# A temperature softmax: the first four-row piece moved to the Scalar queue

## The chip, the cores and the metric

One Trainium2 chip, one of its cores. The metric is the time of one execution in device microseconds, measured on the chip. "Span" is the shorter time that the profile covers, from the core's first to its last instruction (161.2 us where the measured time is 163.27 us). Engines are named as in the profile: DVE is VectorE, ACT is ScalarE, SP is SyncE; SPq and ACTq are the instructions with which SP and ACT issue DMA transfers.

## The reference

The input is 16 x 1024 rows of 512 float32; each row gets a softmax at temperature 0.5.

```python
x_scaled = x / 0.5
x_max = np.max(x_scaled, axis=-1, keepdims=True)
exp_x = np.exp(x_scaled - x_max)
return (exp_x / np.sum(exp_x, axis=-1, keepdims=True)).astype(np.float32)
```

Read once and written once, that is 33.55 MB in and 33.55 MB out.

## The kernel before

The 16,384 rows are cut into 8 tiles of 4 MB: 128 partitions, each with 16 rows (32 KB that lie together in memory). A tile is worked in four blocks of four rows. There are six tile buffers. The first tile is loaded in two pieces, four rows and twelve rows, so that DVE need not wait for the whole tile. All loads are issued by SP, all stores by ACT.

```python
G = 16; B = 4; N_ACT = 1
FIRST = [(0, 4), (4, 16)]
data = ctx.enter_context(tc.tile_pool(name="data", bufs=6))
...
warm = stats.tile([P, 1], fp32, name="warm", bufs=1)     # loads ACT's table early
nc.vector.memset(warm, 0.0)
nc.scalar.activation(out=warm, in_=warm, func=EXP)
...
def load(c):
    xt = tiles[c] = data.tile([P, G, D], fp32, name="xt")
    for lo, hi in FIRST if c == 0 else [(0, G)]:
        nc.sync.dma_start(out=xt[:, lo:hi, :], in_=xr[c][:, lo:hi, :])

def shift(i):          # DVE: row maxima of a block, L65; bias = -2 * max, L67
    ...
def exponentials(i):   # ACT: four times exp(2 x + bias) with row sums, L74
    ...
def scale_vector(i):   # DVE: reciprocal of the sums, L87; three of four rows scaled, L89
    ...
def scale_scalar(i):   # ACT: the fourth row scaled, L95
    ...
def store(i):
    c, b = blocks[i]
    if b + B == G:
        nc.scalar.dma_start(out=outr[c], in_=tiles[c])

for i in range(n + 3):                 # n = 32 blocks
    if i < n:
        if blocks[i][1] == 0:
            load(blocks[i][0])
        shift(i); exponentials(i)
    if 1 <= i <= n:     scale_vector(i - 1)
    if 2 <= i <= n + 1: scale_scalar(i - 2)
    if 3 <= i:          store(i - 3)
```

## Time and profile before

| | before |
|---|---|
| time, median of the first 3 runs | 162.96 us |
| DVE, ACT busy, share of the span | 74%, 71% |
| data moved, mean rate over the span | 67.1 MB, 416 GB/s |
| first maximum on DVE starts | 5.43 us |
| first store issued / last store issued | 34.23 / 144.50 us |

These are the DMA row and the sum line of the page of the kernel before. In the row, each digit is the busy share (tenths, 9 is 90% or more) of one fortieth of the span.

```profile
DMA  5999999998999999999999999999999999999991
HBM read 33.55 MB, written 33.55 MB: 416 GB/s over the span
```

There is no stretch between the first microseconds and the last in which the DMA engines rest. The trace's packet records tell how near to full this is: a 32 KB packet takes 1.213 us, the packet times add up to 156.9 us for each of the 16 engines, and the first data packet starts at 1.76 us and the last ends at 159.94 us. So the engines are busy for 156.9 of 158.2 us.

The waits view of the kernel before (who waited for what: total us, times, longest) says what this means for DVE: it waits for loads.

```profile
DVE negmax L65 <- DMA xt<-in_x_dram: 19.8, 5, 4.8
```

Here is the page's list of DMA issues of the kernel before: destination and source, issuing queue, count, size of each, and the median time from issue to landing. The 1 MB piece lands 4.7 us after its issue.

```profile
xt<-in_x_dram SPq DMA_DIRECT2D x7, 4096.0 KB, 47.3
xt<-in_x_dram SPq DMA_DIRECT2D x1, 3072.0 KB, 11.5
xt<-in_x_dram SPq DMA_DIRECT2D x1, 1024.0 KB, 4.7
```

The timeline of the kernel before has start, duration, engine, line, operation, and in brackets the idle time before it with what ended it. DVE starts block 0 at 5.43 us and then idles 4.79 us for the second piece. The last two lines are the first and the last store.

```profile
5.43 2.29 DVE L65 TENSOR_REDUCE negmax<-xt 128x4 f32<-128x2048 f32 x1 [4.58 <-DMA xt<-in_x_dram]
...
12.71 2.29 DVE L65 TENSOR_REDUCE negmax<-xt 128x4 f32<-128x2048 f32 x1 [4.79 <-DMA xt<-in_x_dram]
...
16.51 2.28 DVE L65 TENSOR_REDUCE negmax<-xt 128x4 f32<-128x2048 f32 x1
...
34.23 0.37 ACTq L102 DMA_DIRECT2D out_dram<-xt  x1
...
144.50 0.34 ACTq L102 DMA_DIRECT2D out_dram<-xt  x1
```

### The profile page before, as it was taken

Reading aid. Unit: us, or ns where it says so; the run is one execution under the profiler, and the core shown is the slowest. Engines: PE = TensorE matmul, PEld = TensorE weight load, DVE = VectorE, ACT = ScalarE, POOL = GpSimd, SP = SyncE. Lnnn points to the kernel's source line nnn. Section 1 sums busy time; section 2 is a strip of 40 time slices with the busy share of each in tenths; the row PEclk is TensorE's granted clock in tenths of the full one; section 3 lists DMA queues with packets and bytes.
Section 4 is the critical chain, followed back from the end, with each engine's and each line's share of the span. In section 5 each row is a group of like instructions: output and inputs, shape, how many; then the busy total and the mean of one; then the engine's idle time right before and its main releaser. Section 6 shows DMA issues by size and latency. Waiting matters only on the chain.

```text
span 161.2 us, 563 instructions
## 1 busy us (share of the span) xinstructions
DVE 119.7 (74%) x193; ACT 114.8 (71%) x290; POOL 0.2 (0%) x4
## 2 busy tenths in 40 slices
DVE  0608999999999999999994999359991799930000
ACT  3072799999999998999995799809997199980000
POOL 0000000000000000000000000000000000000000
DMA  5999999998999999999999999999999999999991
GB/s 193 457 463 447 390 463 447 392 455 317 417 472 398 431 472 398 423 480 398 423 472 409 390 488 423 390 488 423 390 488 423 390 488 425 390 480 431 390 480 65
DMA packets 2452, 67.14 MB, mean 416 GB/s; under 512 B 272, under 2 KB 272, under 8 KB 272
## 3 DMA queue, kind: packets, MB, share of 16 engines
q1 hardware_dynamic: 1296, 33.56, 49.2%
q10 hardware_dynamic: 1152, 33.55, 48.2%
q14 instruction: 4, 0.03, 0.0%
HBM read 33.55 MB, written 33.55 MB: 416 GB/s over the span
## 4 chain that ended last, share of the span: by engine, by line
DMA 54%; DVE 31%; ACT 3%; issue 1%; SPq 0%
DMA xt<-in_x_dram 36%; DVE negmax L65 19%; DMA out_dram<-xt 18%; DVE xt L89 10%; ACT xt L74 2%; DVE bias L67 1%; ACT xt L95 1%; DVE recip L87 1%; SPq L59 0%
## 5 line engine op out<-in xcount | busy, mean ns | idle before, releaser
L74 ACT ACTIVATE xt<-xt,bias 128x512 f32<-128x512 f32 x128 | 90.8, 710 | 28.9 <-DVE bias L67 28.9
L65 DVE TENSOR_REDUCE negmax<-xt 128x4 f32<-128x2048 f32 x32 | 73.0, 2281 | 19.8 <-DMA xt<-in_x_dram 19.8
L89 DVE TENSOR_SCALAR xt<-xt,recip 128x512 f32<-128x512 f32 x96 | 40.9, 483 | 1.1
L74 ACT ACTIVATION_READ_ACCUMULATOR xt<-xt,bias 128x1 f32 x128 | 23.9, 187 | 0.0
L95 ACT ACTIVATE xt<-xt,recip 128x512 f32<-128x512 f32 x32 | 22.4, 706 | 0.0
L87 DVE RECIPROCAL recip<-sums 128x4 f32<-128x4 f32 x32 | 5.5, 171 | 1.6 <-ACT xt L74 1.6
L67 DVE TENSOR_SCALAR bias<-negmax 128x4 f32<-128x4 f32 x32 | 5.5, 170 | 1.1
L50 ACT ACT_TABLE_LOAD x1 | 1.3, 1283 | 0.7 <-PEq L131 0.7
L49 DVE MEMSET warm<- 128x1 f32 x1 | 0.1, 59 | 0.8 <-PEq L131 0.8
L50 ACT ACTIVATE warm<-warm 128x1 f32<-128x1 f32 x1 | 0.2, 203 | 0.0
L131 POOL MEMSET const-bfloat16-1.0<- 128x1 bf16 x1 | 0.1, 101 | 0.0
L131 POOL MEMSET const-uint8-127<- 128x1 uint8 x1 | 0.1, 101 | 0.0
L131 POOL MEMSET const-float32-0.0<- 128x1 f32 x1 | 0.1, 98 | 0.2 <-issue 0.2
L131 POOL MEMSET const-float32-1.0<- 128x1 f32 x1 | 0.1, 98 | 0.0
## 6 DMA issues: line engine op xcount, KB each, us to landing
out_dram<-xt ACTq DMA_DIRECT2D x8, 4096.0 KB, 26.9
xt<-in_x_dram SPq DMA_DIRECT2D x7, 4096.0 KB, 47.3
xt<-in_x_dram SPq DMA_DIRECT2D x1, 3072.0 KB, 11.5
xt<-in_x_dram SPq DMA_DIRECT2D x1, 1024.0 KB, 4.7
```

Source lines behind the costliest of these rows:

```text
L49: nc.vector.memset(warm, 0.0)
L50: nc.scalar.activation(out=warm, in_=warm, func=EXP)
L65: nc.vector.tensor_reduce(negmax, xb, axis=AX, op=MAX, negate=True)
L67: nc.vector.tensor_scalar_mul(bias, negmax, 2.0)
L74: nc.scalar.activation(out=xb[:, g, :], in_=xb[:, g, :], func=EXP, bias=bias[:, g : g + 1], scale=2.0, accum_out=sums[:, g : g + 1],)
L87: nc.vector.reciprocal(recip, sums)
L89: nc.vector.tensor_scalar_mul(xb[:, g, :], xb[:, g, :], recip[:, g : g + 1])
L95: nc.scalar.activation(out=xb[:, g, :], in_=xb[:, g, :], func=COPY, scale=recip[:, g : g + 1])
L131: nc = _bacc.Bacc("TRN2", target_bir_lowering=False, num_devices=1)
```

## The change

The intent: the first piece gets a queue of its own, the Scalar queue, which has nothing to do until the first store; the Sync queue can issue the remainder at once. For that, the first tile's loads are put ahead of the warm-up in the program, so that ACT issues its load before its table load.

```diff
-    warm = stats.tile([P, 1], fp32, name="warm", bufs=1)
-    nc.vector.memset(warm, 0.0)
-    nc.scalar.activation(out=warm, in_=warm, func=EXP)
 ...
         for lo, hi in FIRST if c == 0 else [(0, G)]:
-            nc.sync.dma_start(out=xt[:, lo:hi, :], in_=xr[c][:, lo:hi, :])
+            queue = nc.scalar if (c, lo) == (0, 0) else nc.sync
+            queue.dma_start(out=xt[:, lo:hi, :], in_=xr[c][:, lo:hi, :])
 ...
+    load(0)
+
+    warm = stats.tile([P, 1], fp32, name="warm", bufs=1)
+    nc.vector.memset(warm, 0.0)
+    nc.scalar.activation(out=warm, in_=warm, func=EXP)
+
     n = len(blocks)
     for i in range(n + 3):
         if i < n:
-            if blocks[i][1] == 0:
+            if blocks[i][1] == 0 and i:
                 load(blocks[i][0])
```

## The prediction

> **What bounds the kernel now: the sixteen DMA engines, from about 2 us on.** The page's DMA row shows 9 or more tenths busy in nearly every slice between the first (5) and the last (1); 67.14 MB move at a mean of 416 GB/s over 161.2 us. In the trace's packet records one 32 KB packet takes 1.213 us, so 16 engines move at most 432 GB/s, and 67.1 MB need at least 155 us (my estimate from that duration). The first data packet starts near 1.8 us, the last ends near 160.0 us: only 3 us of slack in DMA. DVE (74% busy) and ACT (71%) have spare time: the waits view shows DVE waiting 19.8 us in total for loads.
>
> **What the change does.** No bytes and no arithmetic are added. One load issue (0.33 to 0.49 us) moves from SP to ACT, ahead of the table load (1.28 us) and the warm-up, which have slack: ACT idles from 2.2 us to block 0's bias at 7.96 us. SP issues the 3 MB remainder about 0.4 us earlier. None of this is on the chain.
>
> The one real effect: before, the 1 MB piece is ahead of the rest in one queue, has all engines and lands 4.7 us after issue; DVE starts block 0 at 5.43 us. After, the 1 MB piece (128 packets of 8 KB) and the 3 MB piece (128 of 24 KB) lie in two queues. The Trainium skill, "DMA: Bandwidth & Descriptors", sections "Queues, rings and completion order" and "Issuing engines are not separate DMA queues", says that both run on the same 16 engines, which take turns packet by packet. The trace agrees: from the first store on, load and store packets interleave at the same total rate. So the small piece loses its priority. My estimate, with 8 and 24 KB packets alternating: it lands at about 11.5 us (8.5 if ACT's packets go in groups first), the remainder near 12.7 us as before, since the sum is the same 4 MB.
>
> DVE then starts block 0 at about 11.5 us; block 1's maximum comes at about 13.8 instead of 12.71 us, and the scale of block 0 waits for four exponentials (2.9 us). DVE runs about 2 us late in the first tiles; the first store is issued at about 36 instead of 34.2 us.
>
> **How much of that is critical: almost nothing.** Six tiles of loads are queued at the start, so the engines stay full until the store comes; loads get 2 us more alone and land earlier later. DVE makes up its lag in its later waits for loads. The last store is issued at 144.5 us but its data cannot start before about 149 us, behind the store before it: over 3 us of slack. Some tenths may come or go at the ramp (first 8 KB packets take up to 0.83 us instead of 0.31).
>
> **Predicted: 162.9 us, 162.2 to 163.9 (8 in 10). Faster by over 2%: 0.01; within 2%: 0.96; slower by over 2%: 0.03.**
>
> **What would show each step.** DMA issues: the 1 MB piece takes near 10 us or more to land instead of 4.7, the 3 MB piece still near 11.5. Timeline: first maximum at 8.5 to 12 us, second at 13 to 14.5; first store issue near 36 us. DMA row unchanged to the end; the last store still over 10 us from issue to landing.
>
> **What would make it wrong.** The DVE lag reaching the last tile and leaving the engines idle before the last store (slower); ACT's queue served first, so that the piece lands early (no lag, same time); two queues costing or saving ramp time.

## More of the kernel before

The end of the chain of waits of the kernel before (start, duration, what) shows the last load, issued at 78.48 us, which DVE gets at 125.80 us.

```profile
78.48 47.30 DMA xt<-in_x_dram
125.80 2.30 DVE negmax L65
```

## The result, and the profile after

The changed kernel takes 163.10 us (median of 4 runs, 162.81 to 163.39), the kernel before in the same rounds 163.06 us (162.91 to 163.21). The ratio is 1.0002, with a 95% interval of 0.998 to 1.0024: the same. Ratios here are the mean time of one kernel's runs over that of the other's of the same rounds, so not quite the ratio of the medians that are quoted beside them. Executions over 1.5% slower than the fastest of the same kernel are left out of the means. A second set of five rounds (below) gave 0.9987.

The time is the same, but the start of the run isn't. These are the DMA issues of the changed kernel.

```profile
xt<-in_x_dram SPq DMA_DIRECT2D x7, 4096.0 KB, 39.9
xt<-in_x_dram SPq DMA_DIRECT2D x1, 3072.0 KB, 12.2
xt<-in_x_dram ACTq DMA_DIRECT2D x1, 1024.0 KB, 12.4
```

The small piece, on a queue of its own, now takes 12.4 us instead of 4.7 us, and lands with the large one. Both were issued at the same moment, as the changed kernel's timeline shows.

```profile
0.72 0.41 ACTq L56 DMA_DIRECT2D xt<-in_x_dram  x1
0.73 2.91 SPq L56 DMA_DIRECT2D xt<-in_x_dram  x6
...
13.12 2.29 DVE L62 TENSOR_REDUCE negmax<-xt 128x4 f32<-128x2048 f32 x1 [12.26 <-DMA xt<-in_x_dram]
...
15.52 2.28 DVE L62 TENSOR_REDUCE negmax<-xt 128x4 f32<-128x2048 f32 x1
...
20.01 2.28 DVE L62 TENSOR_REDUCE negmax<-xt 128x4 f32<-128x2048 f32 x1
...
37.72 0.35 ACTq L99 DMA_DIRECT2D out_dram<-xt  x1
...
141.10 0.34 ACTq L99 DMA_DIRECT2D out_dram<-xt  x1
```

The first maximum starts 7.69 us later, the third 3.50 us later (20.01 against 16.51), the first store 3.49 us later. But the last store is issued 3.40 us earlier. The waits and the end of the chain of the changed kernel say how.

```profile
DVE negmax L62 <- DMA xt<-in_x_dram: 16.0, 2, 12.3
```

```profile
82.52 39.87 DMA xt<-in_x_dram
122.41 2.30 DVE negmax L62
```

DVE's wait for loads falls from 19.8 to 16.0 us, and 12.3 of the 16.0 are now at the start (before, 4.6 + 4.8). The later waits shrink from about 10.4 to 3.7 us. Since the first store came later, the loads had the engines to themselves for longer (by the packet records, 17.9 MB of them had been moved at 50 us, against 17.3 MB before), and the last load was there at 122.41 instead of 125.80 us. The first loss of DVE came back as a shorter wait later on. And the early last store gained nothing either: it takes 19.4 us from issue to landing (15.9 before), because the stores ahead of it are still being moved, and it has landed at 160.5 us (160.4 before).

```profile
DMA  6999999999799999999999999999999999999992
HBM read 33.55 MB, written 33.55 MB: 416 GB/s over the span
```

That is the page of the changed kernel: the same rate, the same full row. (Line 99 of the changed kernel is line 102 of the one before, 62 is 65, 56 is 59.)

The packet records of the trace show how the 16 engines shared the two pieces. This table is counted from them (not a view of the profile): the median end of the Scalar piece's k-th packet over the 16 engines, and how many of Sync's packets each engine had ended by then. (The records do not name the engine: the packets were taken in order of their ends, sixteen to a step, and counts were divided by 16. This holds for all such counts below.)

```
Scalar packet (8 KB)              1     2     3     4     5     6     7     8
ended at, us                   3.85  5.09  6.30  7.51  8.73  9.94 11.16 12.37
Sync packets (24 KB) ended      1.0   2.0   3.0   4.0   5.0   6.0   7.0   8.0
```

One packet of one queue, one of the other, 1.214 us for each such turn (0.912 us for 24 KB and 0.309 us for 8 KB). This is the turn-taking that the Trainium skill states in "DMA: Bandwidth & Descriptors", "Queues, rings and completion order"; the trace agrees, each turn being one of its packet records. A turn is a packet, not a number of bytes: the queue with the smaller packets gets the smaller share, here a quarter.

### The profile page after: what moved, and what is told of

It reads as the page before. It is cut to its first block, busy times and chain, and to the rows that moved or that the text cites. A ratio compares the mean times of both kernels' runs of the same rounds, so it can differ in the third digit from the quotient of the medians.

```text
span 161.4 us, 563 instructions
## 1 busy us (share of the span) xinstructions
DVE 119.5 (74%) x193; ACT 114.7 (71%) x290; POOL 0.2 (0%) x4
## 4 chain that ended last, share of the span: by engine, by line
DMA 51%; DVE 31%; ACT 4%; issue 1%; SPq 0%
DMA xt<-in_x_dram 32%; DVE negmax L62 19%; DMA out_dram<-xt 18%; DVE xt L86 10%; ACT xt L71 3%; DVE bias L64 1%; ACT xt L92 1%; DVE recip L84 1%; SPq L56 0%
## 6 DMA issues: line engine op xcount, KB each, us to landing
xt<-in_x_dram ACTq DMA_DIRECT2D x1, 1024.0 KB, 12.4
```

## The experiments

Two things are to be tested. Why is the piece late: the turns by packet, or something of the Scalar queue, or the moved program text? And why is its lateness free: because the engines are full anyway and the compute has slack (and then how much), or because the change also brought a gain that cancels a loss?

### The order alone

The program order of the change, with both pieces on Sync.

```diff
-            queue = nc.scalar if (c, lo) == (0, 0) else nc.sync
+            queue = nc.sync
```

> The first tile's loads stand ahead of the warm-up in the program, but both pieces stay on the Sync queue. Theory (the queue alone matters, packets of two queues alternate): the 1 MB piece lands 4.7 us after issue and the first maximum starts near 5.4 us as in the kernel before; time 163.0, ratio 1.000 within 0.004. Rival (the early issue, or the warm-up's later place, made the piece late): the piece lands at 10 us or later here too.

The piece landed 4.8 us after issue, as this line from the page of that run shows, and the first maximum started at 5.56 us.

```profile
xt<-in_x_dram SPq DMA_DIRECT2D x1, 1024.0 KB, 4.8
```

So the queue made it late, not the order. The time was 163.40 us against 163.12, ratio 1.0026 (1.0009 to 1.0042), an interval that leaves out 1. So it was run again, with the changed kernel beside it, in five rounds:

> The same kernel as e1_order_only, which came out at 1.0026 with an interval that leaves out 1. Theory (nothing in it can cost 0.4 us; chance of a few runs): ratio 1.000 to 1.002, interval holding 1. Rival (the moved warm-up costs 0.3 us): again 1.002 to 1.004.

> The changed kernel unaltered, in the same rounds as the next run. Theory: the whole change is worth nothing here, ratio 1.000 within 0.003. Against e11_order_again it tells whether the move to the Scalar queue alone, apart from the moved warm-up, costs or gains: theory says under 0.3%.

The order alone: 163.21 us, ratio 1.0000 (0.9986 to 1.0015). The first 0.26% was not repeated, and nothing is built on it. The changed kernel: 163.15 us against 163.25, ratio 0.9987 (0.9969 to 1.0006); two of its six runs were slow (166.12 and 167.35 us) and are left out. In these rounds neither the order alone nor the whole change is worth 0.4%.

### The queues exchanged

```diff
-            queue = nc.scalar if (c, lo) == (0, 0) else nc.sync
+            queue = nc.scalar if (c, lo) == (0, 4) else nc.sync
```

> The 1 MB piece goes on Sync, the 3 MB piece on Scalar. Theory (packet by packet alternation of 8 KB and 24 KB, whichever queue has which): the 1 MB piece is late again, landing 10.5 to 12.5 us after issue; the 3 MB piece 12 to 13. Rival (the Scalar queue is served later or slower than Sync): the 1 MB piece lands early, near 5 us, and the 3 MB piece is late, at 13 us or more. Time near 163 under both.

```profile
xt<-in_x_dram ACTq DMA_DIRECT2D x1, 3072.0 KB, 12.5
xt<-in_x_dram SPq DMA_DIRECT2D x1, 1024.0 KB, 12.3
```

The 1 MB piece, on Sync, took 12.3 us; the 3 MB piece, on Scalar, 12.5 us. The Scalar queue is not served worse: the small piece is late on either, as soon as the large one is on the other. (163.61 us, one run.)

The packet records of this run show one thing more. Here the small piece's packet came first in each turn, and its eighth had ended at 11.49 us (median over the engines), 0.9 us sooner than in the changed kernel. Yet it landed hardly sooner. Each transfer here ends with a packet of 4 bytes on every engine, and those of the small piece started only at 12.06 to 12.66 us, 0.90 to 0.91 us after its last data packets: the time of one more packet of 24 KB. So this last small packet waited for a turn of its own.

### Equal packets

```diff
-    FIRST = [(0, 4), (4, 16)]
+    FIRST = [(0, 4), (4, 8), (8, 12), (12, 16)]
```

> As the changed kernel, but the 3 MB remainder on Sync is three pieces of 1 MB, so that packets of both queues are 8 KB. Theory (alternation by packet, so bytes are shared in proportion to packet size): the Scalar piece lands after 16 packets of 0.309 us per engine, 7 to 8.5 us after the start instead of 13.1; first maximum at 7.5 to 8.5 us. Rival (the Scalar queue waits until Sync's first tile is through): still near 13 us. Time 163 under both, 162.3 to 163.8.

The Scalar piece took 7.6 us; the first maximum started at 8.31 us. With packets of 8 KB in both queues the Scalar piece gets half of the bytes instead of a quarter: its eighth packet ended at 7.46 us, with exactly 8 Sync packets ended on each engine. (163.36 us, one run.)

### Small packets

The same 1 MB, issued on Scalar as four loads of one row each, so with packets of 2 KB.

```diff
-    FIRST = [(0, 4), (4, 16)]
+    FIRST = [(0, 1), (1, 2), (2, 3), (3, 4), (4, 16)]
...
-            queue = nc.scalar if (c, lo) == (0, 0) else nc.sync
+            queue = nc.scalar if c == 0 and lo < 4 else nc.sync
```

> As the changed kernel, but the Scalar piece is four loads of one row each: 32 packets of 2 KB per engine instead of 8 of 8 KB, the same 1 MB. Theory (one packet per turn, whatever its size): the 32 packets need 32 turns beside Sync's 8 packets of 24 KB and 24 of 32 KB, so the last row lands near 40 us (36 to 44); compute starts then, past the slack that ends near 23.7 us: time 178 to 183 us. Rival (queues share bytes, or Scalar is served in bulk): the piece lands by 13 us or earlier and the time stays 163.

These are the first maximum and the last store in the timeline of that run.

```profile
42.93 2.29 DVE L62 TENSOR_REDUCE negmax<-xt 128x4 f32<-128x2048 f32 x1 [42.08 <-DMA xt<-in_x_dram]
...
167.06 0.34 ACTq L99 DMA_DIRECT2D out_dram<-xt  x1
```

DVE sat idle for 42.08 us waiting for 1 MB. The 32nd Scalar packet ended at 41.7 us, when each engine had ended 31.75 Sync packets: one for one again, but now with 24 KB and then 32 KB on the other side of each turn. The time is 182.09 us against 163.20, ratio 1.1149 (1.1127 to 1.117). The same idea as the change, with another packet size, costs 11%.

### Sync a little later

If the turns decide, a lead for Scalar should help. First, Sync's first load waits for a DVE memset of a 128x2048 scratch tile (through a memset of one element of each partition in the part to be loaded).

```diff
         xt = tiles[c] = data.tile([P, G, D], fp32, name="xt")
+        if c == 0:
+            nc.vector.memset(xt[:, 4, 0:1], 0.0)
...
+    scratch = stats.tile([P, B, D], fp32, name="scratch", bufs=1)
+    nc.vector.memset(scratch, 0.0)
     load(0)
```

> As the changed kernel, but Sync's first load waits for a DVE memset of a 128x2048 scratch tile [...], so the Scalar piece has the engines alone for that long. Theory: each of its 8 packets per engine sent alone saves one alternation round (0.91 + 0.31 = 1.22 us): landing 6 to 11 us instead of 12.4, the earlier the later Sync's first packet. Rival (Scalar is served only after Sync): still 12 us or more. Time unchanged near 163 (162.3 to 164), since the engines have the Scalar piece to work on meanwhile.

Sync's issue came at 3.02 us (the memset took 1.76 us), and the piece landed after 4.8 us, outside the 6 to 11 that were expected. The lead seemed to be too long: Sync's first packet started at 4.67 us, when about seven of each engine's eight Scalar packets had ended on average. So it was run with a quarter of the memset.

```diff
-    nc.vector.memset(scratch, 0.0)
+    nc.vector.memset(scratch[:, 0, :], 0.0)
```

> As e8_sync_later with a quarter of the scratch memset, so that Sync's first load is issued about 1.3 us later than it would be (near 1.7 to 2.1 us) and its first packet comes when some of the Scalar piece's 8 packets per engine have gone. Theory (alternation): each packet gone alone saves one turn of 1.22 us; with 1 to 4 gone the piece lands 8 to 12 us after issue, between the 4.8 of e8 and the 12.4 of the changed kernel. Rival (one queue is served before the other, all or nothing): 5 or 12.5. Time near 163.

These lines are from the timeline of that run.

```profile
0.72 0.38 ACTq L58 DMA_DIRECT2D xt<-in_x_dram  x1
...
1.42 2.93 SPq L58 DMA_DIRECT2D xt<-in_x_dram  x6
...
5.63 2.29 DVE L64 TENSOR_REDUCE negmax<-xt 128x4 f32<-128x2048 f32 x1 [4.23 <-DMA xt<-in_x_dram]
```

The piece landed after 4.9 us, not after 8 to 12. This expectation failed, and it corrects the theory. Sync's issue was only 0.70 us behind Scalar's. In the kernel before and in the changed one the first packet came about 1.0 us after the first issue (0.73 to 1.76 us, 0.72 to 1.73 us), so Sync's could have come near 2.5 us. It came at 4.57 us. On each engine it came right behind Scalar's last: the sixteen first Sync packets start 4 to 6 ns after the sixteen 4-byte packets that end Scalar's transfer. A fixed delay after the issue is not the reason: Sync's first packet came 3.15 us after its issue here, 1.65 us in the run with the longer lead. The reading that fits is that alternation does not begin when the second queue has work: what the engines have by then taken from the first queue goes first. This is inferred; the trace does not show what an engine has taken and not yet started. In the changed kernel the issues are 0.01 us apart, and there one Sync packet went ahead and then strict turns followed; 0.70 us of lead was enough for all eight packets.

The stores agree with this reading. In the kernel before, the first store is issued at 34.23 us and its first packet starts at 38.64 us; in the 4.41 us between, each engine ends three load packets of 32 KB. In the run with small packets the engines had run out of loads when the first store came (67.53 us), and its first packet started after 0.87 us. How deep this is, and whether it is counted in packets or bytes, no run here tells. The time of both runs with a lead was unchanged (163.01 and 162.94 us, one run each).

### The whole first tile at once

The kernel before, without any early piece.

```diff
-    FIRST = [(0, 4), (4, 16)]
+    FIRST = [(0, 16)]
```

> The kernel before with its first tile loaded whole, in one DMA of 4 MB on Sync: no early piece at all. Theory: the first maximum starts near 13 us, the first store near 37.7, as in the changed kernel; the lag is absorbed and the time is 163.0, ratio 1.000 within 0.004. Rival (the early first piece is worth its 7 us, or part of it): 165 or more.

The first maximum started at 13.02 us, about as in the changed kernel. Three runs took 162.97 to 163.09 us, the fourth, the profiled one, 165.20 us (not counted as slow, being less than 1.5% above the others). The median is 163.06 us, the ratio 1.0021 (0.9975 to 1.0067). Three of the four runs say that the early piece, which the kernel before has 7.6 us sooner (5.43 against 13.02), is worth nothing in time; the interval allows up to 0.7%.

### Late compute, early loads

To measure the slack, the kernel before gets useless work on DVE ahead of block 0, with all loads as they were: seven extra maxima of a scratch tile, or fourteen.

```diff
     nc.scalar.activation(out=warm, in_=warm, func=EXP)
+    scratch = stats.tile([P, B, D], fp32, name="scratch", bufs=1)
+    nc.vector.memset(scratch, 0.0)
+    dump = stats.tile([P, B], fp32, name="dump", bufs=1)
+    for _ in range(7):      # 14 in the second
+        nc.vector.tensor_reduce(dump, scratch, axis=AX, op=MAX, negate=True)
```

> The kernel before, with a scratch memset and seven extra 128x2048 maxima (2.28 us each) on DVE before block 0: the compute starts near 18 us instead of 5.43, the loads as before. Theory (DMA-bound, compute lag absorbed): the last store may be issued near 143 to 146 us, the engines stay full, time 163.0, within 0.6. Rival (a late start is on the critical path, and the change's lag was paid for by some gain elsewhere): time longer by several us, up to 12.

> The same with fourteen extra maxima: compute starts near 34 us. Theory: the slack ends when the start passes about 23.7 us (last store issued 124.8 us after the compute start, when DVE never waits, and 11.5 us more until it has landed, against an end at 160 us); 34 is about 10 us past that: time 172.5 us, 170 to 175. Rival (compute lag is always absorbed, DMA bytes alone set the time): 163.

With seven, the first maximum started at 19.18 instead of 5.43 us, and the time was 163.09 us, ratio 0.9986 (0.9966 to 1.0005).

```profile
19.18 2.27 DVE L71 TENSOR_REDUCE negmax<-xt 128x4 f32<-128x2048 f32 x1
...
143.31 0.34 ACTq L108 DMA_DIRECT2D out_dram<-xt  x1
```

So 13.75 us of compute lag cost nothing, and nothing of the change is in this kernel that could have cancelled it. The last store was issued at 143.31 us, and took 16.9 us to land.

With fourteen, the time was 174.54 us, ratio 1.0691 (1.0669 to 1.0712). This is the DMA row of its page, and below it the first maximum and the last store in its timeline.

```profile
DMA  6999899999989898499989999999998588089995
```

```profile
35.43 2.27 DVE L71 TENSOR_REDUCE negmax<-xt 128x4 f32<-128x2048 f32 x1
...
159.52 0.34 ACTq L108 DMA_DIRECT2D out_dram<-xt  x1
```

Now there are holes in the row (4 in the middle, 5 and 0 near the end): the engines run dry because the stores come late. In this run and in the two other late ones (seven maxima, small packets) the last store is issued 124.1 us after the first maximum: 35.43 to 159.52, 19.18 to 143.31, 42.93 to 167.06. This is the pipeline without any further wait for loads. In the two of these runs that lost time, the last store takes 12.3 us to land, and in the kernel before it has landed at 144.50 + 15.9 = 160.4 us. So the compute may start as late as 160.4 - 12.3 - 124.1 = 24.0 us. The times of the two runs beyond it agree: 174.54 - 163.20 = 11.34 us lost for a start at 35.43, which puts the free limit at 24.1; 18.89 us lost for 42.93, which puts it at 24.0. Between these two runs beyond the limit, 7.50 us of later start cost 7.55 us; at 19.18 us no loss was measured, and no run lies between 19.18 and 35.43 us.

### Late loads

The counterpart: the first load, and with it all others on Sync, waits for the scratch memset and two extra maxima.

```diff
+    scratch = stats.tile([P, B, D], fp32, name="scratch", bufs=1)
+    nc.vector.memset(scratch, 0.0)
+    dump = stats.tile([P, B], fp32, name="dump", bufs=1)
+    for _ in range(2):
+        nc.vector.tensor_reduce(dump, scratch, axis=AX, op=MAX, negate=True)
...
         xt = tiles[c] = data.tile([P, G, D], fp32, name="xt")
+        if c == 0:
+            nc.vector.memset(xt[:, 0, 0:1], 0.0)
```

> The kernel before, with its first load (and so all loads) waiting for a scratch memset and two extra maxima on DVE: first issue near 6.5 to 7 us instead of 0.73. Theory (idle DMA time at the start is paid in full, unlike idle compute time): time longer by the same 6 us: 169 us, 168 to 170. Rival (anything at the start is absorbed): 163.

These are the first issue in the timeline of that run, and the DMA row of its page.

```profile
7.70 3.50 SPq L67 DMA_DIRECT2D xt<-in_x_dram  x7
```

```profile
DMA  0099999999999999999999999999999999999991
```

The first issue came at 7.70 instead of 0.73 us, 6.97 us later, and the time was 170.17 against 163.20 us, 6.97 us longer (ratio 1.0415, 1.0391 to 1.0438). The time was just above the 168 to 170 that were expected, because the issue came later than the 6.5 to 7 us that were assumed. The start of the run is not free as such. Idle time of the DMA engines there is paid in full; idle time of DVE is not.

## Why the prediction was right

- **The time.** Predicted 162.9 us and "within 2%", measured 163.10 us. The reason given was that the DMA engines bound the kernel. The late loads (6.97 us in, 6.97 us out) and the late compute (13.75 us in, nothing out) show it from both sides. The agreement to 0.2 us says nothing of the sizes that the prediction gave to the lag and to the slack, since any lag within the slack leaves the same time.
- **The piece loses its priority.** Right, and the mechanism, turns by packet, is shown by the packet count, the exchanged queues, the equal packets and the small packets. The size was off: it landed at 13.1 us (12.4 us after its issue), where 11.5 us was estimated. The estimate has the small piece land 1.2 us, one turn, ahead of the remainder; in fact both landed together, at 13.1 and 12.9 us. In the changed kernel Sync's packet came first in each turn, so the small piece's data ended with the last packet of the large one. But the order in a turn is not the whole of it: with the queues exchanged the small piece's data ended a turn sooner, at 11.49 us, and its 4-byte last packet still waited for the large piece's last. The first Sync packet of nearly every engine was also slow, 1.1 to 1.8 us instead of 0.912.
- **The DVE lag.** Predicted as about 2 us with the first store near 36 us; it was 3.5 us, with the first store at 37.72 us. The first two maxima, at 13.12 and 15.52 us, lay outside the ranges given (8.5 to 12 and 13 to 14.5). Most of this is the same mis-sized term, carried on.
- **The lag is absorbed.** Right in its mechanism: the last load landed 3.4 us earlier, and DVE's later waits shrank by 6.7 us (10.4 to 3.7), about the 3.5 us of the lag and these 3.4 us together. The slack at the end was put at "over 3 us" from the last store alone. That was correct as a lower bound (its 15.9 us to landing against 12.3 us) but missed the greater part, since waits for loads also give way. By that figure alone a lag of 3.5 us would have been close to the limit. Measured from the compute's start, the slack is 24.0 - 5.4 = 18.6 us, of which the change uses 7.7. But the kernel before waits 4.8 us for its second piece anyway. At the first store, which comes 24.6 us after the first maximum when nothing is waited for, the slack is 24.0 + 24.6 - 34.2 = 14.4 us, and the change uses 3.5.
- **"ACT's packets in groups first"** was named as a possible case. It is what happens when ACT's issue leads by 0.70 us, and it did not happen in the change.

No version here is shown to beat the kernel before. Its engines are busy for 156.9 us of the 158.2 us in which data move, so less than 1% is left in that stretch.

## What to carry to other kernels

A transfer that must be early is best kept ahead of the others in one queue, or given a clear lead (0.70 us was enough here, in one run): on a second queue it takes turns with everything else, packet for packet, and the smaller its packets the longer it waits (the same 1 MB was there for DVE at 13.1 us in 8 KB packets, and at 42.9 us in 2 KB packets). Before an early start of the compute is bought, measure what a late one costs: put useless work ahead of it and find the point from which time is lost. In a kernel whose DMA engines are always full, only bytes and idle DMA time count, and a loss at the start of the compute that stays within the slack, here 7.7 us, leaves no trace in the time.

## What the Trainium skill lacked or had wrong

- "DMA: Bandwidth & Descriptors", "Queues, rings and completion order", says that engines take turns by packet, which the runs confirm. It does not say what this does to a small transfer: 1 MB took 4.7 us ahead in one queue, 12.4 us on a queue of its own in 8 KB packets, and in 2 KB packets DVE waited 42.08 us for it. It also speaks of packets of some 9 to 17 descriptors; the turns seen here were single packet records of 2, 8 or 24 KB, one partition's contiguous rows each. Nor does it say that the packet of 4 bytes with which a transfer ends waits for a turn too: with the queues exchanged it came 0.9 us after the small piece's last data, the time of one more packet of 24 KB.
- No section of that page tells how long a newly arrived queue waits behind work already taken from another (the reading inferred above): a lead of 0.70 us let eight 8 KB packets pass, and a first store waited 4.41 us behind three 32 KB load packets, against 0.87 us with the engines free.
- The same page, "Where 436 GB/s comes from", says without a condition that the HBM side, some 358 GB/s, binds transfers between HBM and SBUF. Here 67.1 MB moved in 158.2 us, 424 GB/s, on one core, which fits the page's own 425 GB/s for a 16 MB load. The page's section "Bandwidth" has the condition that is missing there: about 358 GB/s is each core's part when both cores of an HBM domain stream. Every run here used one core.
- The same page, "Issuing engines are not separate DMA queues", says that issuing from several engines only saves the issue time. Here the 3 MB piece was issued 0.42 us sooner (0.73 against 1.15 us), which saved nothing in the time (ratio 1.0002), and the order of landing changed; the section doesn't mention the order.
